# A forgetting-attention layer whose q and k are transposed by VectorE and DMA, in a two-block kernel on one Trainium2 core

## The chip, the core and the metric

The kernel runs on one core of a Trainium2 chip. The metric is device microseconds of one execution, over the whole program. TensorE is called PE in the rows, its weight loads PEld, VectorE DVE, ScalarE ACT, GpSimd POOL and SyncE SP.

## What is computed

A sequence of 256 positions by 1024 channels (float32) goes through five stages. Each weight matrix is used once.

```
x = x + 0.5 * swiglu_ffn(rmsnorm(x, ffn1_norm), ...)          # 1024 -> 2816 -> 1024
x = x + hybrid_mixer(rmsnorm(x, mix_norm), ...)               # 8 heads of 64, banded; and pooling
x = x + 0.5 * swiglu_ffn(rmsnorm(x, ffn2_norm), ...)
x = rmsnorm(x, final_norm)
x = layer_norm(ALPHA * x + fox_mixer(x), ln_g[0], ln_b[0])    # 8 heads of 128, forgetting
x = layer_norm(ALPHA * x + dsa_mixer(x), ln_g[1], ln_b[1])    # 8 heads of 128, indexed top-k
```

The mixer that matters most here, with `scale = 128 ** -0.5`:

```
q, k, v, f_logit, gate = split(x @ w_in)
cum = cumsum(log_sigmoid(f_logit + b_f))            # one decay per head and position
s = q k^T * scale + cum[q] - cum[k], causal
out = (silu(gate) * softmax(s) v) @ w_out
```

## The kernel before, in words

The 256 positions are two tiles (t = 0, 1) of 128 partitions. The activations stand transposed in `xT`, as a high and a low part whose sum is the float32 value. A weight product is therefore three products on PE (`half`, L215): high by high, low by high, high by low. The weights come in 236 units of two blocks of 128 rows and up to 512 columns, in the order of the list `UNITS`. SyncE loads a unit into one of four `raw` buffers (L204), ScalarE casts it to `whi` (L197) and VectorE subtracts to get `wlo` (L198); up to eight units are split ahead of their use.

A chunk (`chunk`, L338) is up to 512 output columns: for each tile 24 products accumulate in one of four PSUM banks called `mm`. Small work is put between the products. `later(us, fn)` and `when(keys, us, fn)` (L136, L140) put a function into a heap with a due time, in a count of PE time (`now`, L168), and each `half` ends by running what is due (`pump`). The due times are in `DUE` (L86). The framework's scheduler sets the final order on every engine, which then works in order.

**Start** (`start`, L1107). Twenty-eight products of zeros (L1120) are issued on PE before the first weights are there.

**Feed-forward layers** (L371). Their hidden values are transposed without PE: VectorE transposes blocks of 32×32 (`hb`, L413), POOL's DMA queue writes `hb` to DRAM in four parts and reads it back as one tile `hd` with the blocks in place (`regroup`, L276), and ScalarE and VectorE make the parts `hh`, `hl` (L239, L240) 9.5 us of counted time later.

**Mixer** (L470). Its four chunks are the pool inputs, k, q and v. The scores of tile 0 (L528) alternate between the heads on partitions 0-63 and 64-127 (`e` = 0, 1). After the softmax each `e` is handled alone: `pv` (L545) transposes its p (four transposes on PE and one copy), and `pv2` (L549) multiplies it with v, 64 columns of v to one half of the output's partitions:

```
for i in range(nh):
    for k in range(nk // P):
        self.mm(aT[t][64 * e:64 * e + 64, j, :], v[k][...], pT[:, i, k, :], ...)
```

The output is then split (`oa`), and products on it follow those on the pool half (`op`).

**Forgetting layer** (`fox`, L687). Its chunks are k (two), the decays with the first part of v, q (two), the rest of v (two), and the gates (in `attend`, L843, where tile 0 goes first). At the layer's start SyncE loads four rows, repeated over 128 partitions: `b_f`, `final_norm`, `ln_g0`, `ln_b0` (L700 to L702). `xT` already holds the normed x up to its row factor, which the evacuations apply (`rs`); x itself, wanted again only in the layer norm at the end, is normed in place right after chunk 0 (L730). In chunk 0 the second half of `xT` is still being made, tile by tile: four transposes on PE, then `xg` on VectorE (L244), a cast on ScalarE (L245), `xl` on VectorE (L246). Each evacuated q or k chunk (`y`, L708) is transposed by PE, four blocks of 128×128 (L713), 1.57 us later; VectorE copies tile 0 (L716) and the parts are made from PSUM (L718). The decays (`cums`, L751) go to DRAM and come back as a row for all partitions on POOL's queue, and POOL adds the causal mask twice (L771, L772). Tile 0's scores use the plain copies (L800), tile 1's the parts.

Of the kernel before, what the change touches and what calls it, by code (L numbers as in the profile page):

```python
# [31 lines left out]
N_WARM = 28  # L32
# [14 lines left out]
def unit_list():  # L47
# [48 lines left out]
    "fox_T": 1.57,  # L96
# [18 lines left out]
class Kern:  # L115
# [332 lines left out]
    def p_T(self, pool, s, nh, nk, split=False):  # L448
# [15 lines left out]
        out = pool.tile([P, 512], F32, name="pT", bufs=2)  # L464
        self.flip = not getattr(self, "flip", False)
        (self.nc.scalar.copy if self.flip else self.nc.vector.tensor_copy)(out, ps)
        return out.rearrange("p (h k q) -> p h k q", h=nh, q=P)


    def mixer(self, u, gain, next_gain):  # L470
        self.stage = "mix"
        nc, tc, A = self.nc, self.tc, self.A
        with tc.tile_pool(name="mix", bufs=1, reuse_waits="tile") as pool:
# [46 lines left out]
            def scores(t, b):  # L520
# [3 lines left out]
                for i in range(nh):  # L524
                    for e in range(2):
                        j, r = nh * b + i, slice(64 * e, 64 * e + 64)
                        if t == 0:
                            self.mm(ps[e][:, i, :], qT[r, j, :], kT[r, j, :], True, True)  # L528
                        else:
                            self.mm3(ps[e][:, i, :], qTs, kTs, True, True, (r, j), (r, j))  # L530
                for e in range(2):
                    s = pool.tile([P, nh, nk], F32, name="s", bufs=6)
                    h0 = 2 * nh * b + e
# [7 lines left out]
                    self.when([("mix", "v")], DUE["mix_pv"], lambda e=e, s=s: pv(t, b, e, s, nh, nk))  # L541
# [3 lines left out]
            def pv(t, b, e, s, nh, nk):  # L545
                pT = self.p_T(pool, s, nh, nk)
                self.later(DUE["mix_pv2"], lambda: pv2(t, b, e, pT, nh, nk))

            def pv2(t, b, e, pT, nh, nk):  # L549
                if b == e == 0:  # L550
# [6 lines left out]
                if e == 1 and nh * (b + 1) == 4:  # L557
# [99 lines left out]
    def silu_gate(self, pool, acc, out, hr):  # L657

        nc = self.nc
        th = pool.tile([P, 512], F32, name="th", bufs=2)  # L660
# [26 lines left out]
    def fox(self, u, gain):  # L687
        self.stage = "fox"
        nc, tc, A = self.nc, self.tc, self.A
        with tc.tile_pool(name="fox", bufs=1, reuse_waits="tile") as pool:  # L690
            kT, qT = (pool.tile([P, 8, P], F32, name=n) for n in ("kT", "qT"))
# [7 lines left out]
            ck0 = pool.tile([P, 8, P], F32, name="ck0")  # L699
# [6 lines left out]
            def qk(acc, t, whole, part, h0, scale):  # L706
# [12 lines left out]
                self.later(DUE["fox_T"], go)  # L719

            def qk_chunks(js):
                nonlocal u
                for j in js:
                    for t, acc in self.chunk(u, 4, gain if j == 0 else None):
                        if j == 0:
# [4 lines left out]
                            nc.vector.scalar_tensor_tensor(self.x[t], self.x[t], rs[t], fg,  # L730
                                                           op0=ALU.mult, op1=ALU.mult)
                        if j < 2:
                            qk(acc, t, kT, [d[:, :, t * P:(t + 1) * P] for d in kTs], 4 * j, rs[t])
                        else:
                            qk(acc, t, qT, qTs if t else None, 4 * j - 8, sr[t])
# [15 lines left out]
            def cums():  # L751
# [12 lines left out]
                nc.scalar.activation(cs, ps[0:8, 0:S], AF.Copy, scale=-1.0)  # L764
                d = self.dp.tile([8, S], F32, name="ck")
# [27 lines left out]
            def scores(t, g):  # L793
# [3 lines left out]
                for i in range(nh):  # L797
                    h = g * nh + i
                    if t == 0:
                        self.mm(ps[:, i, :], qT[:, h, :], kT[:, h, :], True, True)  # L800
                    else:
                        self.mm3(ps[:, i, :], qTs, kTs, True, True, (slice(None), h), (slice(None), h))
                    nc.vector.scalar_tensor_tensor(s[:, i, :], ps[:, i, :], cq[t][:, h:h + 1],
                                                   (ck if t else ck0)[:, h, :], op0=ALU.add, op1=ALU.add)
# [29 lines left out]
            def after(t, o):  # L834
                self.layer_norm(t, o, lg, lb)
# [7 lines left out]
    def attend(self, u, pool, gt, hr, scores, pv):  # L843
# [13 lines left out]
        for t in range(2):  # L857
# [10 lines left out]
            self.open_xT(t)  # L868

# [14 lines left out]
    def dsa(self, u, x_gain=None):  # L884
        self.stage = "dsa"
        nc, tc, A = self.nc, self.tc, self.A
        with tc.tile_pool(name="dsa", bufs=1, reuse_waits="tile") as pool:
# [202 lines left out]
            for t, g in GROUPS:  # L1090
                ql = [("dsa", "ql", i) for i in ((2 * g, 2 * g + 1) if t == 0 else (g,))]
                self.when([("dsa", "sel", t)] + ql, 0.0, lambda t=t, g=g: self.fire(("dsa", "k", t, g)))
            self.attend(u, pool, gt, [None, None], scores, pv)
# [141 lines left out]
```

## Time and profile before

| | |
|---|---|
| median of the runs shown (3) | 724.43 us (723.4 to 725.69) |
| the profiled execution | 723.93 us, span of the profile 722.1 us |
| PE busy | 706.5 us (98%) |
| VectorE, ScalarE busy | 492.1 us (68%), 369.4 us (51%) |
| POOL busy | 62.3 us (9%) |
| moved by DMA | 140.87 MB, 195 GB/s over the span |

The span runs from the first to the last instruction that the profile records; the execution's own time is 1.8 us longer. Matmuls are pipelined and their ends are modelled, so the start of one to the start of the next is the better measure of a product than its duration.

### The profile page before, as it was taken

What the parts mean: (1) busy time and instruction counts of PE and PEld (TensorE: products, weight loads), DVE (VectorE), ACT (ScalarE), POOL (GpSimd) and SP (SyncE); (2) the same over time, 40 slices, a digit from 0 to 9 for tenths busy, and PEclk for the clock granted to TensorE, in tenths of its full rate; (3) what the DMA queues carried; (4) which work ended last, traced back from release to release, by engine and by line L of the source; (5) the groups of instructions that cost most, each with busy time, mean ns of one, the idle gap of its engine ahead of it and who ended that gap; (6) DMA issues with size and microseconds to landing.
All of it is one profiled execution on the core that took longest, in us unless ns stands there. A gap on an engine that the chain in (4) does not pass through costs nothing.

```text
span 722.1 us, 9816 instructions
## 1 busy us (share of the span) xinstructions
PE 706.5 (98%) x3580; PEld 593.9 (82%) x3580; DVE 492.1 (68%) x790; ACT 369.4 (51%) x552; POOL 62.3 (9%) x90
## 2 busy tenths in 40 slices
PE   8999999999999999999999999999999999999995
PEld 7788889888888778888889888778898888778984
DVE  5776765575647867666776575556456968997965
ACT  6654544454545645454454354446464635675820
POOL 0101110300001001011110300000300001000001
PEclk9999999999999999999999999999999999999998
DMA  8898666875734425668765885546572527633501
GB/s 253 305 317 309 212 215 208 285 266 188 271 122 167 154 94 181 202 199 288 228 224 196 270 265 189 196 142 195 169 248 101 156 63 251 206 118 117 175 1 59
DMA packets 42305, 140.87 MB, mean 195 GB/s; under 512 B 5512, under 2 KB 6672, under 8 KB 42128
## 3 DMA queue, kind: packets, MB, share of 16 engines
q1 hardware_dynamic: 37728, 127.23, 52.7%
q0 software_dynamic: 4096, 12.60, 5.1%
q8 instruction: 28, 0.46, 0.2%
q10 hardware_dynamic: 432, 0.41, 0.2%
q14 instruction: 21, 0.17, 0.1%
HBM read 133.39 MB, written 6.82 MB: 194 GB/s over the span
## 4 chain that ended last, share of the span: by engine, by line
PE 88%; DVE 5%; DMA 3%; ACT 2%; issue 1%; SPq 0%; POOL 0%; DVEq 0%; POOLq 0%; ACTq 0%
PE mm L164 79%; PE sc L164 5%; PE tr L179 3%; DVE wlo L198 2%; DMA raw<-in_w 1%; DMA row_final_norm<-in_final_norm 1%; PE tr L164 1%; ACT whi L197 1%; DMA xin<-in_xT 1%; ACT s L445 0%; DVE sel L983 0%; DVE xl L317 0%; DVE sel L992 0%; DVE s L534 0%; POOL hrs L292 0%
## 5 line engine op out<-in xcount | busy, mean ns | idle before, releaser
L198 DVE TENSOR_TENSOR wlo<-raw,whi 128x1024 fp32r<-128x1024 f32 (+3 forms) x236 | 274.6, 1178 | 84.8 <-ACT whi L197 74.9
L197 ACT CAST whi<-raw 128x1024 fp32r<-128x1024 f32 (+3 forms) x236 | 235.7, 1014 | 126.0 <-PE mm L164 76.4
L164 PE MATMUL mm<-whi,xh 128*128 128x512 f32 (+3 forms) x760 | 289.3, 381 | 1.7 <-ACT whi L197 1.6
L164 PE MATMUL mm<-whi,xl 128*128 128x512 f32 (+3 forms) x760 | 284.9, 375 | 2.2 <-DVE xl L246 2.2
L164 PE MATMUL mm<-wlo,xh 128*128 128x512 f32 (+3 forms) x760 | 284.0, 375 | 0.1
L164 PEld LDWEIGHTS mm<-whi,xh 128*128 128x128 f32 x760 | 144.0, 189 | 25.7 <-ACT whi L197 3.0
L164 PEld LDWEIGHTS mm<-whi,xl 128*128 128x128 f32 x760 | 144.2, 190 | 25.0 <-DVE xl L246 2.7
L164 PEld LDWEIGHTS mm<-wlo,xh 128*128 128x128 f32 x760 | 143.9, 189 | 25.3 <-DVE wlo L198 1.3
L164 PE MATMUL mm<-whi,hh 128*128 128x512 f32 x176 | 68.7, 390 | 0.0
L164 PE MATMUL mm<-whi,hl 128*128 128x512 f32 x176 | 68.5, 389 | 0.0
L164 PE MATMUL mm<-wlo,hh 128*128 128x512 f32 x176 | 68.5, 389 | 0.0
L240 DVE TENSOR_TENSOR hl<-hd,hh 128x512 fp32r<-128x512 f32 (+1 forms) x24 | 14.5, 644 | 53.3 <-ACT hh L239 53.3
L239 ACT CAST hh<-hd 128x512 fp32r<-128x512 f32 (+1 forms) x24 | 12.8, 583 | 60.9 <-DMA hd<-d 60.9
L282 POOL DMA_DIRECT2D d<-hb x48 | 26.5, 559 | 149.9 <-DVE hb L413 136.3
L164 PEld LDWEIGHTS mm<-wlo,hh 128*128 128x128 f32 x176 | 33.0, 188 | 6.9
L164 PEld LDWEIGHTS mm<-whi,hh 128*128 128x128 f32 x176 | 33.1, 188 | 6.7
L164 PEld LDWEIGHTS mm<-whi,hl 128*128 128x128 f32 x176 | 33.1, 188 | 6.7
L400 ACT ACTIVATE th<-mm,hr 128x512 f32<-128x512 f32 (+1 forms) x24 | 15.6, 648 | 25.2 <-PE mm L164 24.1
L445 ACT ACTIVATE s<-s,nmax 128x128 f32<-128x128 f32 (+1 forms) x48 | 21.3, 446 | 7.0 <-DVE nmax L443 7.0
L292 POOL TENSOR_TENSOR rs<-ms,mhalf 128x1 f32<-128x1 f32 x10 | 6.5, 653 | 175.4 <-DVE ms L305 175.4
L402 DVE SCALAR_TENSOR_TENSOR a<-th,mm 128x512 f32<-128x512 f32 (+1 forms) x24 | 15.2, 632 | 8.5 <-ACT th L400 8.5
L292 POOL TENSOR_TENSOR lr<-ve,mhalf 128x1 f32<-128x1 f32 x4 | 4.0, 992 | 167.8 <-DVE ve L640 167.8
(219 smaller groups left out, 602.0 us busy)
## 6 DMA issues: line engine op xcount, KB each, us to landing
raw<-in_w SPq DMA_DIRECT2D x208, 512.0 KB, 4.5
d<-hb POOLq DMA_DIRECT2D x40, 128.0 KB, 4.8
hd<-d POOLq DMA_DIRECT2D x10, 512.0 KB, 6.6
raw<-in_w SPq DMA_DIRECT2D x12, 344.0 KB, 3.6
raw<-in_w SPq DMA_DIRECT2D x8, 372.0 KB, 3.6
raw<-in_w SPq DMA_DIRECT2D x8, 256.0 KB, 4.4
x<-in_x SPq DMA_DIRECT2D x2, 512.0 KB, 6.3
B<-in_bias SPq DMA_DIRECT2D x1, 1024.0 KB, 7.0
```

What stands on the lines that cost most here:

```text
L164: self.nc.tensor.matmul(out, a, b, start=start, stop=stop)
L179: self.nc.tensor.transpose(out, a, self.ident[:p, :p])
L197: nc.scalar.copy(hi[:, :m], raw[:, :m])
L198: nc.vector.tensor_sub(lo[:, :m], raw[:, :m], hi[:, :m].bitcast(F32))
L239: nc.scalar.copy(hi, src)
L240: nc.vector.tensor_sub(lo, src, hi.bitcast(F32))
L282: self.nc.gpsimd.dma_start(out=d[a].rearrange("b i m -> i b m"), in_=src[32 * a:32 * a + 32])
L292: self.nc.gpsimd.tensor_tensor(out, a, self.mhalf[:, 0:1].to_broadcast(list(a.shape)), op=ALU.pow)
L400: nc.scalar.activation(th[:, :w], acc[:, :w], AF.Tanh, scale=hr[t])
L402: nc.vector.scalar_tensor_tensor(a[t][:, :w], th[:, :w], 1.0, acc[:, :w], op0=ALU.add, op1=ALU.mult)
L445: nc.scalar.activation(s[:, h, :], s[:, h, :], AF.Exp, bias=m[:, h:h + 1], accum_out=l[:, col + h:col + h + 1])
```

## The change

In the forgetting layer q and k take the way of the feed-forward layers' hidden values: VectorE transposes the evacuated `y` in 32×32 blocks into `yb`, POOL's queue regroups it into `yT` (one buffer for each k chunk, one that both q chunks share), and 12 us of counted time later one function makes what PE's transposes had fed. Tile 0's scores read k from `yT` directly. The final norm of x is put off by 9 us of counted time. Several buffers are shared in time: `final_norm` with `ck0`, `ln_g0` and `ln_b0` with the two `yT` of k, so these two rows are loaded after tile 0's gates (`between`); `pT` with `yb`, `th` with `y`. In the mixer both `e` of a group are handled together, and their products with v alternate. The start has 42 products of zeros.

```diff
-N_WARM = 28
+N_WARM = 42
...
-    "fox_T": 1.57,
+    "fox_T": 12.0,
+    "fox_norm": 9.0,
...
-                    self.when([("mix", "v")], DUE["mix_pv"], lambda e=e, s=s: pv(t, b, e, s, nh, nk))
+                self.when([("mix", "v")], DUE["mix_pv"], lambda: pv(t, b, ss, nh, nk))
...
+            def pv(t, b, ss, nh, nk):
+                pT = [self.p_T(pool, s, nh, nk, bufs=4) for s in ss]
+                self.later(DUE["mix_pv2"], lambda: pv2(t, b, pT, nh, nk))
...
                 for i in range(nh):
                     j = nh * b + i
                     for k in range(nk // P):
-                        self.mm(aT[t][64 * e:64 * e + 64, j, :], v[k][:, 128 * j + 64 * e:128 * j + 64 * e + 64],
-                                pT[:, i, k, :], k == 0, k == nk // P - 1)
+                        for e in range(2):
+                            self.mm(aT[t][64 * e:64 * e + 64, j, :], v[k][:, 128 * j + 64 * e:128 * j + 64 * e + 64],
+                                    pT[e][:, i, k, :], k == 0, k == nk // P - 1)
...
-            fg = self.row(pool, "final_norm")
-            lg, lb = self.row(pool, "ln_g0"), self.row(pool, "ln_b0")
+            fg = self.row(pool, "final_norm", tag="ck0")
...
+            def qk(acc, t, j, scale):
                 y = pool.tile([P, 512], F32, name="y", bufs=2)
                 nc.scalar.activation(y, acc, AF.Copy, scale=scale)
+                if t == 0:
+                    self.yb = pool.tile([P, 4, 256], F32, name="yb", bufs=2)
+                nc.vector.transpose(self.yb[:, :, t * P:(t + 1) * P].rearrange("p b (c j) -> p b c j", c=4),
+                                    y.rearrange("p (c b j) -> p b c j", c=4, b=4))
+                if t == 0:
+                    return
+                yT[j] = pool.tile([P, 4, 256], F32, name=f"yT{j}" if j < 2 else "yTq")
+                self.regroup(yT[j], self.yb)
+                hs = slice(4 * (j % 2), 4 * (j % 2) + 4)
                 def go():
-                    ps = self.bank("tr")
-                    for i in range(4):
-                        self.tr(ps[:, i * P:(i + 1) * P], y[:, i * P:(i + 1) * P])
-                    pv_ = ps.rearrange("p (i q) -> p i q", i=4)
-                    if t == 0:
-                        nc.vector.tensor_copy(whole[:, h0:h0 + 4, :], pv_)
-                    if part is not None:
-                        self.split_psum(*(d[:, h0:h0 + 4, :] for d in part), pv_)
+                    for tt in range(2):
+                        v = yT[j][:, :, tt * P:(tt + 1) * P].rearrange("p a (c j) -> p c a j", c=4)
+                        if j >= 2 and tt == 0:
+                            nc.scalar.copy(qT[:, hs, :].rearrange("p c (a j) -> p c a j", a=4), v)
+                            continue
+                        part = [d[:, hs, tt * P:(tt + 1) * P] for d in kTs] if j < 2 else [d[:, hs, :] for d in qTs]
+                        self.split_psum(*(d.rearrange("p c (a j) -> p c a j", a=4) for d in part), v)
                 self.later(DUE["fox_T"], go)
...
-                            nc.vector.scalar_tensor_tensor(self.x[t], self.x[t], rs[t], fg,
-                                                           op0=ALU.mult, op1=ALU.mult)
+                            self.later(DUE["fox_norm"], lambda t=t: nc.vector.scalar_tensor_tensor(
+                                self.x[t], self.x[t], rs[t], fg, op0=ALU.mult, op1=ALU.mult))
...
+            rows = []
+            self.between = lambda: rows.extend((self.row(pool, "ln_g0", tag="yT0"), self.row(pool, "ln_b0", tag="yT1")))
             self.attend(u, pool, gt, hr, scores, pv)
```

## Rows read from the trace of the kernel before

**Rows 1.** The page: an engine's busy time, and the chain that ended last by engine.
```profile
PE 706.5 (98%) x3580; PEld 593.9 (82%) x3580; DVE 492.1 (68%) x790; ACT 369.4 (51%) x552; POOL 62.3 (9%) x90
PE 88%; DVE 5%; DMA 3%; ACT 2%; issue 1%; SPq 0%; POOL 0%; DVEq 0%; POOLq 0%; ACTq 0%
```
**Rows 2.** The longest of PE's waits: us in total, times, longest.
```profile
PE mm L164 <- DVE xl L246: 2.2, 1, 2.2
```
**Rows 3.** Timeline at the forgetting layer's start: start, us, what, [idle before <- releaser].
```profile
467.78 0.48 PE L164 MATMUL mm<-whi,xh 128*128 128x512 f32 x1
468.54 1.28 DVE L730 SCALAR_TENSOR_TENSOR x<-x,rs,row_final_norm 128x1024 f32<-128x1024 f32 x1 [2.74 <-DMA row_final_norm<-in_final_norm]
469.75 0.69 DVE L246 TENSOR_TENSOR xl<-xg,xh 128x512 fp32r<-128x512 f32 x1
470.49 0.80 PE L164 MATMUL mm<-whi,xl 128*128 128x512 f32 x1 [2.23 <-DVE xl L246]
473.92 0.39 PE L164 MATMUL mm<-whi,xh 128*128 128x512 f32 x1
```
**Rows 4.** Stretches: length; busy us (count) of PE, PEld, DVE, ACT, POOL; clock; DMA share; GB/s.
```profile
467.80:470.50 2.70, 0.47 (x5) 0.16 (x2) 1.96 (x3) 0.36 (x1) 0.00 (x0) 0.97 0.85 338
470.50:473.90 3.40, 3.40 (x8) 2.71 (x9) 3.40 (x5) 0.62 (x1) 0.00 (x0) 0.52 0.52 172
474.00:496.00 22.00, 22.00 (x118) 19.19 (x117) 10.80 (x15) 12.17 (x17) 0.00 (x0) 1.00 0.52 166
615.00:720.00 105.00, 97.99 (x565) 83.04 (x563) 86.62 (x226) 54.38 (x109) 2.84 (x4) 0.98 0.34 114
```
**Rows 5.** The chain in the forgetting layer's projections: one group of transposes.
```profile
519.59 0.44 PE tr L179 x4
```
**Rows 6.** The mixer: timeline of PE, the chain (start, us, what), a stretch.
```profile
258.13 1.09 PE L164 MATMUL sc<-pT,v 128*64 128x128 f32 x8
235.86 1.16 PE L164 MATMUL sc<-kT,qT 64*128 64x128 f32 x16
...
255.41 1.51 PE sc L164 x16
...
262.50:267.15 4.65, 4.65 (x22) 3.86 (x21) 3.44 (x4) 3.67 (x5) 0.00 (x0) 1.00 0.15 33
```
**Rows 7.** The kernel's start: timeline of PE, two stretches, the chain.
```profile
1.01 3.17 PE L1120 MATMUL tr<-zero 128*128 128x128 bf16 x28 [1.01 <-DVE zero L1139]
5.27 0.79 PE L164 MATMUL mm<-whi,xh 128*128 128x512 f32 x1 [1.09 <-ACT whi L197]
...
5.30:9.45 4.15, 4.15 (x10) 3.28 (x11) 2.73 (x7) 2.65 (x8) 0.00 (x0) 1.00 0.95 304
18.50:22.85 4.35, 3.59 (x13) 2.02 (x13) 3.39 (x6) 3.14 (x4) 0.00 (x0) 1.00 0.98 386
...
14.22 6.20 DMA raw<-in_w
```
**Rows 8.** First feed-forward layer: last transpose, writes, the cast that waits; PE beside.
```profile
59.71 0.71 DVE L413 STREAM_TRANSPOSE hb<-h 128x512 f32<-128x512 f32 x1
60.72 2.19 POOL L282 DMA_DIRECT2D d<-hb  x4 [17.25 <-DVE hb L413]
73.08 1.14 ACT L239 CAST hh<-hd 128x512 fp32r<-128x512 f32 x2 [6.80 <-DMA hd<-d]
...
66.10:73.10 7.00, 7.00 (x33) 5.79 (x32) 1.45 (x2) 0.20 (x2) 0.76 (x1) 1.00 0.85 328
```
**Rows 9.** The gathered tile hd: its reads' time from issue to landing.
```profile
DMA to landing us min/median/max: 3.1/6.3/7.7
```
**Rows 10.** Timeline: the decays' last addition, the last q, tile 0's last scores.
```profile
517.45 2.40 POOL L772 TENSOR_TENSOR ck<-ck,cst 128x1024 f32<-128x1024 f32 x1
...
523.28 0.68 ACT L708 ACTIVATE y<-mm,qr 128x512 f32<-128x512 f32 x1
...
544.17 0.63 PE L164 MATMUL sc<-kT,qT 128*128 128x128 f32 x4
```

More of the change, by code (lines that the diff above doesn't have):

```diff
@@ L446, in softmax_part, with p_T @@
                                  accum_out=l[:, col + h:col + h + 1])
-    def p_T(self, pool, s, nh, nk, split=False):
+    def p_T(self, pool, s, nh, nk, split=False, bufs=2):
         ps = self.bank("tr")
@@ L463, in p_T @@
                 self.tr(v[:, h, k, :], s[:, h, k * P:(k + 1) * P])
-        out = pool.tile([P, 512], F32, name="pT", bufs=2)
+        out = pool.tile([P, 512], F32, name="pT", tag="yb" if self.stage == "fox" else "pT", bufs=bufs)
         self.flip = not getattr(self, "flip", False)
@@ L530, in scores @@
                             self.mm3(ps[e][:, i, :], qTs, kTs, True, True, (r, j), (r, j))
+                ss = []
                 for e in range(2):
                     s = pool.tile([P, nh, nk], F32, name="s", bufs=6)
+                    ss.append(s)
                     h0 = 2 * nh * b + e
@@ L540, in scores, with pv2 @@
                         nc.vector.tensor_scalar(s[:, i, :], s[:, i, :], ri[:, i:i + 1], None, op0=ALU.mult)
-                    self.when([("mix", "v")], DUE["mix_pv"], lambda e=e, s=s: pv(t, b, e, s, nh, nk))
+                self.when([("mix", "v")], DUE["mix_pv"], lambda: pv(t, b, ss, nh, nk))
             aT = {}
[L545 to L550, printed above, removed]
+            def pv(t, b, ss, nh, nk):
+                pT = [self.p_T(pool, s, nh, nk, bufs=4) for s in ss]
+                self.later(DUE["mix_pv2"], lambda: pv2(t, b, pT, nh, nk))
+            def pv2(t, b, pT, nh, nk):
+                if b == 0:
                     aT[t] = self.bank("sc").rearrange("p (i q) -> p i q", i=4)
@@ L554, in pv2 @@
                     for k in range(nk // P):
-                        self.mm(aT[t][64 * e:64 * e + 64, j, :], v[k][:, 128 * j + 64 * e:128 * j + 64 * e + 64],
-                                pT[:, i, k, :], k == 0, k == nk // P - 1)
-                if e == 1 and nh * (b + 1) == 4:
+                        for e in range(2):
+                            self.mm(aT[t][64 * e:64 * e + 64, j, :], v[k][:, 128 * j + 64 * e:128 * j + 64 * e + 64],
+                                    pT[e][:, i, k, :], k == 0, k == nk // P - 1)
+                if nh * (b + 1) == 4:
                     self.split_psum(*oT[t, "a"], aT[t])
@@ L659, in silu_gate @@
         nc = self.nc
-        th = pool.tile([P, 512], F32, name="th", bufs=2)
+        th = pool.tile([P, 512], F32, name="th", tag="y" if self.stage == "fox" else "th", bufs=2)
         nc.scalar.activation(th, acc, AF.Tanh, scale=0.5 if hr is None else hr)
@@ L690, in fox @@
         with tc.tile_pool(name="fox", bufs=1, reuse_waits="tile") as pool:
-            kT, qT = (pool.tile([P, 8, P], F32, name=n) for n in ("kT", "qT"))
+            yT = {}
+            qT = pool.tile([P, 8, P], F32, name="qT")
             kTs, qTs = self.parts(pool, [P, 8, S], "kTs"), self.parts(pool, [P, 8, P], "qTs")
@@ L764, in cums @@
                 nc.scalar.activation(cs, ps[0:8, 0:S], AF.Copy, scale=-1.0)
+                ck0 = self.ck0 = pool.tile([P, 8, P], F32, name="ck0", tag="ck0")
                 d = self.dp.tile([8, S], F32, name="ck")
@@ L803, in scores @@
                     nc.vector.scalar_tensor_tensor(s[:, i, :], ps[:, i, :], cq[t][:, h:h + 1],
-                                                   (ck if t else ck0)[:, h, :], op0=ALU.add, op1=ALU.add)
+                                                   (ck if t else self.ck0)[:, h, :], op0=ALU.add, op1=ALU.add)
                 self.softmax_part(pool, s, nh, nk, l[t], g * nh)
@@ L834, in after @@
             def after(t, o):
-                self.layer_norm(t, o, lg, lb)
+                self.layer_norm(t, o, *rows)
                 if t == 0:
@@ L868, in attend @@
             self.open_xT(t)
+            if t == 0:
+                self.between()
     def gate_out(self, t, hb, o, l, f, gt):
@@ L1092, in dsa @@
                 self.when([("dsa", "sel", t)] + ql, 0.0, lambda t=t, g=g: self.fire(("dsa", "k", t, g)))
+            self.between = lambda: None
             self.attend(u, pool, gt, [None, None], scores, pv)
```

9 lines of the change are left out of this document (4 added, 5 removed).

## The prediction

> **What bounds the kernel now.** I read the page first. The product engine (PE) is busy 98% of the span of 722.1 us, and the chain that ended last is 88% PE [rows 1]: time can go only where PE waits, runs at the lower clock, or does something that can be left out. PE's list of waits comes next; the longest, 2.2 us, is a weight product that waits for VectorE's xl [rows 2]. The timeline shows why. At the start of the forgetting layer VectorE stands 2.74 us before the final norm of x (L730), because the row of gains is still landing. The norm takes 1.28 us, and only behind it comes xl, for which PE stands [rows 3]. Then the clock: in the next 3.4 us it is 0.52 of full, 1.2 instead of 2.4 GHz, after a stretch in which PE was busy 0.47 of 2.70 us [rows 4]. I then looked up the other operations that the change touches: the transposes by PE [rows 5], the mixer's products with v [rows 6], the first 23 us [rows 7], and the way by VectorE and DMA, which the feed-forward layers already use [rows 8, 9].
>
> The sum is made against the profiled execution's own 723.93 us, which is 0.50 under the median of the runs shown, 724.43; I add 0.5 at the end. About 0.3% (2.2 us) is what a measurement of this kernel can tell from no change.
>
> **1. Final norm put off.** The norm leaves VectorE's queue between xg and xl, and with it the wait for the row. xl then follows its cast and is done before the product that needs it, which starts one step after 467.78. A step is 0.228 us, so it starts at 468.01 instead of 470.49: 2.48 us of standing go. From 470.49 to 473.92 are eight steps in 3.43 us; at 0.228 each they are 1.82, so the low clock cost 1.61 [rows 3]. Together **−4.09**. Late next is tile 1's xl: its transposes end at about 468.0, then xg, cast and xl at 0.69 or less each, so 470.1; it is needed twelve products after 467.78, at 470.5. It fits, barely. The two norms come about 9 us later, beside weight products, where VectorE is busy 10.80 of 22 us [rows 4]: nothing. The rows ln_g0 and ln_b0 leave SP's queue at the layer's start and stand in it between weight loads, after the gates of tile 0. Their buffers are those of k, last read by tile 0's scores, at 544 [rows 10]; SP is behind that, so it does not wait, and the weights behind it lie eight units ahead. Nothing.
>
> **2. q and k transposed by VectorE and DMA.** Removed from PE: eight groups of four transposes, 0.44 us each on the chain [rows 5]: **−3.5**. VectorE loses four copies and gets eight transposes of 0.71 [rows 8], at most 5.7 us in a stretch of some 60 in which it is half idle [rows 4]: hidden by PE's products. ScalarE gets two copies of q, about 0.6 each like the cast of the gathered tile [rows 8]: hidden too. POOL gets 16 writes and 4 reads, and their way is the term to bound. In the feed-forward layer the last transpose starts at 59.71, the writes are issued from 60.72, and ScalarE starts on the result at 73.08: 13.4 us, 14.1 with an evacuation of 0.68 before it. ScalarE stood 6.8 us for it, and PE did not stand: busy 7.00 of 7.00 us [rows 8], since the weights are cast eight units ahead. In the new place k has all the time it needs. The last q is the close one: its evacuation starts at 523.28 and its score products at 544.17 [rows 10], 20.9 us later, 20.4 with one group of transposes gone. Against 14.1 that leaves 6 us. But POOL is also busy with the row of decays until 519.85 [rows 10]. If the first q queues behind that, it lands 12.4 later (60.72 to 73.08), at 532. The two q share one buffer, so the second read waits for the first's parts, some 2.5 us: issued at 535, it lands by the median of 6.3 us [rows 9] at 541, copied by 542. Slack 1.5 us or more. Bounds: 0; or, with the longest landing of 7.7 [rows 9] at each of three transfers, a stand of 1 to 3 us and the clock's fall after it, together 4. I take **0**: the nearest row is ScalarE's wait of 6.8 us, which cost PE nothing.
>
> A rule speaks against this part. The Trainium skill, VectorE: DVE Perf Modes, Rules for kernel authors, gives a 128×128 transpose to TensorE if it may end in PSUM. By that rule the 3.5 would be no gain, and the sum would be 717.7. On the rows PE is the scarce engine and VectorE half idle there, so I go by the rows.
>
> **3. Heads take turns at v.** There are 24 products of 128×64 by 128 columns, recorded as 48 instructions. One group of eight, all to the same 64 partitions, lasts 1.09 us [rows 6]. After the change neighbours write partitions 0-63 and 64-127. Two rows are near. The scores of tile 0 use row halves in turn, and sixteen last 1.16 us, hardly more than eight. And where now two groups with v meet, one to the upper and one to the lower half, sixteen take 1.51 on the chain [rows 6], though two groups alone would take two times 1.09: where they meet, column halves seem to run beside each other. So I take half of the steps away: a step within a group is about 0.11 us ((1.09 − 0.3) / 7), 24 × 0.11 = **−2.6**. Bounds: 0 if neighbours don't overlap in this order; −3.0 if fewer changes between kinds of products save too. Is PE the limit there? After the last product with v PE is busy 4.65 of 4.65 us with products on the pool half, before those on the attention half begin [rows 6]; the split that these wait for is a cast and a subtraction, under 1.4 us. So PE is the limit, with 3 us of cover.
>
> **4. 42 warming products.** 28 take 3.17 us, so fourteen more take 1.6 and end at 5.8, where the first weight product now starts at 5.27 after a gap of 1.09: 0.5 late. If the low clock ended earlier, the ten products until 9.45 would save 0.2 each [rows 7]. Neither reaches the end: the chain from 14 to 20.4 is one weight transfer of 6.20 us, with the DMA engines 98% busy, and PE is busy only 3.59 of 4.35 us before 22.85 [rows 7]: it stands for weights anyway. **0**; bounds +0.5 and −1.
>
> Sum: −4.09 − 3.5 − 2.6 = −10.2; 723.93 − 10.2 = 713.7; with 0.5 added **714.2 us**. Later stages only shift: in the last 105 us the DMA engines are busy 0.34 [rows 4], and what VectorE does there starts with PE's products.
>
> **The rivals.**
> *Column halves don't overlap in this order.* Against it stands the group of sixteen. Part 3 is 0: 716.8. Chance 0.06.
> *The last q lands late.* One stand before the scores of tile 0, priced like the one at the layer's start, 4.09: 718.3. For it: POOL's queue and the single buffer; against: 1.5 us of slack and gate products that can go first. Chance 0.16.
> *The earlier clock counts.* PE has a gap before 5.27 and ten products at the lower clock after it. If the clock rose earlier and an earlier PE brought the next transfers forward, the 0.8 us that PE stands before 22.85 would go: 713.4. Against: that chain holds no product. The Trainium skill, TensorE: Matmul & The Clock Gate, What's actually happening, says that activity releases the lower clock; no row here shows it rise sooner. Chance 0.04.
> *Nothing arrives.* The norm is put off, but its row or the gathered parts stop VectorE again at the same cost: 723 to 725. Chance 0.03.
> *Slower.* Place: ScalarE's queue in the projections. The parts of q and k stand in it from their due time on; if each waits longer than the weights are cast ahead, PE stands four times, at 4.09 each +16.4: 730.6. Eight units of six products at 0.228 are 11 us; with the 12 of the due time that decides at a landing 23 us after the evacuation, and I count 14 to 18. Chance 0.07.
>
> **How the numbers follow.** My forecast has 0.64; its own range is 712.5 to 716. The range reaches over the columns and a late q, 711.8 to 719.5; the last two rivals and the edges are left out. Faster by over 0.3%: 0.64 + 0.06 + 0.16 + 0.04 = 0.90; within: 0.03; slower: 0.07.
>
> **What would show it.** Right: no wait for xl at the layer's start and a clock of 1.00 there; no transposes of y on PE; the sixteen products of a pair with v in about 1.1 us; casts of q and k that wait for a gather while PE goes on. Wrong: a wait of PE for qT before tile 0's scores, v's products still 0.11 apart, VectorE standing for the gains' row in another place, or a later stage that now waits where it did not.

## The result, and the profile after

The kernel after the change takes 728.32 us (median of 6 runs), the kernel before 723.91 on the same chip: ratio 1.0063, 95% interval 1.0037 to 1.0088. It is 4.4 us slower where 10.2 faster was forecast. Its profiled execution took 729.85 us (span 728.1), 1.5 above its median.

The page shows it first: PE is busy 2.7 us less, as its transposes of q and k are gone and the mixer's products overlap, but it is a smaller part of the chain, 72% instead of 88% [rows 1].

```profile
PE 703.8 (97%) x3562; PEld 589.6 (81%) x3562; DVE 497.5 (68%) x794; ACT 368.5 (51%) x554; POOL 74.5 (10%) x110
PE 72%; DMA 12%; DVE 7%; ACT 3%; issue 3%; POOL 2%; SPq 0%; DVEq 0%; POOLq 0%; ACTq 0%
```

PE's list of waits after (total, times, longest) is headed by two waits that were not there before [rows 2]; both are of tile 0's scores in the forgetting layer.

```profile
PE sc L165 <- ACT qT L729: 4.9, 1, 4.9
PE sc L165 <- DVE s L819: 1.8, 1, 1.8
PE mm L165 <- DVE a L403: 1.7, 2, 1.0
PE mm L165 <- ACT whi L198: 1.7, 2, 1.3
PE mm L165 <- DVE xl L247: 1.3, 1, 1.3
```

**Where the time went.** The table takes the start of one and the same instruction in two traces and gives what each stage took more (+) or less than in the trace of before. The stages end, in the time of before, with the first feed-forward layer (190.8), the mixer (279.9), the second feed-forward layer (461.7), the first evacuated k (474.9), the second tile's decay logits (498.3), the last evacuated q (523.3), the last gate of the forgetting layer (573.1) and the last x (713.7). The ratio is the measured one, to the kernel before on the same chip, with its 95% interval; it can differ a little from that of the two medians. e1 to e18 are the experiments; each has one trace, and where its profiled execution lies above or below the median, so does the sum of its row.

| | median | ratio | ffn1 | mixer | ffn2 | first k | decays | last q | last gate | rest |
|---|---|---|---|---|---|---|---|---|---|---|
| after | 728.32 | 1.0063 (1.0037-1.0088) | +1.7 | -2.5 | +1.4 | -2.4 | -1.7 | -1.7 | **+11.3** | +0.6 |
| e1 | 717.89 | 0.9930 (0.9906-0.9954) | 0.0 | -2.5 | +1.1 | -2.4 | -1.6 | -0.3 | 0.0 | +2.2 |
| e2 | 724.25 | 1.0021 (1.0001-1.0041) | -0.5 | -2.5 | +1.4 | -2.6 | -1.7 | -1.7 | +8.2 | +1.0 |
| e3 | 720.92 | 0.9971 (0.9952-0.9989) | -1.3 | -2.5 | +2.5 | -0.2 | 0.0 | 0.0 | 0.0 | +0.4 |
| e4 | 724.09 | 1.0018 (1.0003-1.0034) | +0.1 | 0.0 | 0.0 | -0.3 | 0.0 | 0.0 | 0.0 | +0.3 |
| e5 | 725.36 | 1.0021 (1.0002-1.0040) | +1.1 | -2.6 | 0.0 | -2.4 | -1.6 | -1.7 | +9.1 | +0.3 |
| e6 | 728.77 | 1.0067 (1.0048-1.0085) | +1.0 | -2.5 | 0.0 | -2.5 | -1.7 | -1.7 | +11.3 | +1.0 |
| e7 | 720.81 | 0.9960 (0.9941-0.9979) | +0.2 | -2.5 | 0.0 | -2.4 | -1.7 | -1.7 | +4.5 | +2.6 |
| e8 | 717.52 | 0.9906 (0.9873-0.9938) | +2.4 | -2.5 | 0.0 | -4.0 | -2.3 | +0.3 | 0.0 | +0.8 |
| e9 | 715.99 | 0.9906 (0.9881-0.9931) | -0.5 | -2.5 | +0.6 | -4.0 | -2.1 | +0.2 | +0.4 | +1.1 |
| e10 | 718.20 | 0.9931 (0.9906-0.9956) | +3.7 | -2.5 | 0.0 | -4.0 | -2.3 | +0.3 | 0.0 | +2.1 |
| e11 | 721.52 | 0.9975 (0.9956-0.9994) | +0.4 | 0.0 | 0.0 | -4.0 | -0.1 | -0.1 | 0.0 | +2.6 |
| e12 | 717.04 | 0.9917 (0.9888-0.9946) | +2.0 | -2.5 | 0.0 | -4.0 | -2.3 | -1.1 | +2.6 | +2.1 |
| e13 | 724.31 | 1.0013 (0.9995-1.0031) | +1.9 | 0.0 | 0.0 | -2.6 | +0.2 | 0.0 | 0.0 | +1.2 |
| e14 | 724.03 | 1.0000 (0.9985-1.0015) | +0.1 | 0.0 | 0.0 | -2.4 | +0.2 | 0.0 | 0.0 | 0.0 |
| e15 | 717.59 | 0.9919 (0.9888-0.9950) | +3.3 | -2.5 | 0.0 | -4.0 | -2.0 | -1.2 | +0.4 | +1.2 |
| e16 | 727.16 | 1.0041 (1.0021-1.0061) | +2.5 | -2.5 | 0.0 | -2.1 | -1.7 | -1.7 | +10.6 | +2.1 |
| e17 | 724.77 | 1.0014 (0.9994-1.0034) | +1.7 | -2.5 | 0.0 | -2.3 | -1.6 | -1.4 | +10.4 | +0.8 |
| e18 | 723.77 | 0.9990 (0.9965-1.0014) | +1.8 | -2.5 | 0.0 | -4.0 | -1.8 | -1.2 | +8.7 | +1.4 |

Read the first row: by the last q the change is 5.2 us ahead, though it began 1.7 behind; then 11.3 us go in one stage. What stands in the first column is mostly chance: e8 and e10 are one and the same kernel and differ by 1.2 there.

**The stage that loses.** Timelines after (start, us, what, [idle before <- releaser]): POOL, then ScalarE and VectorE, then PE.

```profile
509.08 0.57 POOL L283 DMA_DIRECT2D d<-yb  x1 [0.61 <-DVE yb L717]
513.92 2.39 POOL L786 TENSOR_TENSOR ck<-ck,cst 128x1024 f32<-128x1024 f32 x1 [4.27 <-DMA ck<-ck]
516.28 3.02 POOL L787 TENSOR_TENSOR ck<-ck,cst 128x1024 f32<-128x1024 f32 x1
519.25 1.65 POOL L283 DMA_DIRECT2D d<-yb  x3
526.39 0.76 POOL L284 DMA_DIRECT2D yTq<-d  x1 [5.49 <-DMA d<-yb]
534.10 0.76 POOL L284 DMA_DIRECT2D yTq<-d  x1 [4.78 <-DVE qTsl L241]
...
531.94 0.62 ACT L729 COPY qT<-yTq 128x512 f32<-128x512 f32 x1 [8.76 <-DMA yTq<-d]
539.84 1.04 ACT L198 CAST whi<-raw 128x1024 fp32r<-128x1024 f32 x1 [2.10 <-DMA raw<-in_w]
541.41 1.04 ACT L198 CAST whi<-raw 128x1024 fp32r<-128x1024 f32 x1 [0.52 <-DMA raw<-in_w]
542.36 0.61 ACT L729 COPY qT<-yTq 128x512 f32<-128x512 f32 x1
...
544.90 1.22 DVE L199 TENSOR_TENSOR wlo<-raw,whi 128x1024 fp32r<-128x1024 f32 x1 [0.59 <-ACT whi L198]
546.05 0.60 DVE L819 SCALAR_TENSOR_TENSOR s<-sc,cq,ck 128x128 f32<-128x128 f32 x2
...
535.34 0.50 PE L165 MATMUL mm<-wlo,xh 128*128 128x512 f32 x1 [0.53 <-DVE wlo L199]
537.73 0.38 PE L165 MATMUL sc<-yT,qT 128*128 128x128 f32 x2
543.02 0.79 PE L165 MATMUL sc<-yT,qT 128*128 128x128 f32 x2 [4.91 <-ACT qT L729]
546.44 1.22 PE L165 MATMUL sc<-yT,qT 128*128 128x128 f32 x4 [1.77 <-DVE s L819]
```

Three of the first q's four writes stand on POOL behind the decays' additions; its read goes out at 526.39. ScalarE stands 8.76 us for it, in front of the casts of the weights that come next. When it goes on, the weights are late in turn: it waits 2.10 and 0.52 us for raw ones, and the copy of the last q, which had landed by 538.5 (issued at 534.10, 4.4 us, the tile's own row below), stands behind these casts until 542.36. PE stands from 538.1. Then the additions of the first scores stand on VectorE behind a low part of weights (544.90), and PE stands once more. The chain that ended last runs through the same pieces (start, us, what):

```profile
526.39 5.52 DMA yTq<-d
533.08 0.96 ACT whi L198
535.21 1.23 DVE wlo L199
536.45 4.86 DMA raw<-in_w
541.41 1.04 ACT whi L198
546.05 0.35 DVE s L819
546.44 1.22 PE sc L165 x4
```

So the weights that come late were asked for late: a load waits until a buffer of raw weights has been cast and subtracted, and SyncE issued none between 524.46 and 535.31. In 530 to 535 the DMA engines were busy 0.40, in the kernel of e1, which has no such stand, 0.77. Stretches and tile (columns as in [rows 4]):

```profile
DMA to landing us min/median/max: 4.4/5.0/5.5
...
538.10:543.00 4.90, 0.01 (x1) 0.00 (x0) 2.64 (x3) 2.64 (x4) 0.00 (x0) 0.83 0.98 374
543.00:551.00 8.00, 6.20 (x21) 5.10 (x22) 4.77 (x10) 3.84 (x5) 0.00 (x0) 0.50 0.62 205
```

PE stands 4.9 + 1.8 us, and 0.5 before them for a low part of weights; from 543 it works 6.20 us at half the clock, which at full clock would be some 3.1. Together 10.3 of the 11.3.

**The layer's start** (against [rows 3]): tile 0's norm is still between xg and xl.

```profile
468.17 1.28 DVE L744 SCALAR_TENSOR_TENSOR x<-x,rs,row_final_norm 128x1024 f32<-128x1024 f32 x1 [1.85 <-DMA row_final_norm<-in_final_norm]
469.38 0.69 DVE L247 TENSOR_TENSOR xl<-xg,xh 128x512 fp32r<-128x512 f32 x1
470.12 0.50 PE L165 MATMUL mm<-whi,xl 128*128 128x512 f32 x1 [1.34 <-DVE xl L247]
```

**The mixer and the first 23 us** (against [rows 6, 7]): sixteen products of a pair with v last what eight did; the first weight product is at the full clock, and PE stands for weights as before.

```profile
256.79 1.09 PE L165 MATMUL sc<-pT,v 128*64 128x128 f32 x16
...
6.03 0.50 PE L165 MATMUL mm<-whi,xh 128*128 128x512 f32 x1 [0.42 <-ACT whi L198]
...
18.50:22.85 4.35, 3.46 (x14) 2.52 (x15) 2.96 (x3) 2.69 (x4) 0.00 (x0) 1.00 1.01 383
```

### The profile page after: what moved, and what is told of

Its sections match the earlier page's. It is cut to its first block, busy times and chain, and to the rows that moved or that the text cites. A ratio compares the mean times of both kernels' runs of the same rounds, so it can differ in the third digit from the quotient of the medians.

```text
span 728.1 us, 9833 instructions
## 1 busy us (share of the span) xinstructions
PE 703.8 (97%) x3562; PEld 589.6 (81%) x3562; DVE 497.5 (68%) x794; ACT 368.5 (51%) x554; POOL 74.5 (10%) x110
## 4 chain that ended last, share of the span: by engine, by line
PE 72%; DMA 12%; DVE 7%; ACT 3%; issue 3%; POOL 2%; SPq 0%; DVEq 0%; POOLq 0%; ACTq 0%
PE mm L165 63%; PE sc L165 5%; DMA raw<-in_w 5%; DVE wlo L199 3%; PE tr L180 3%; DMA hd<-d 2%; DMA d<-hb 2%; ACT whi L198 2%; DMA ck<-ck 1%; POOL d L283 1%; PE tr L165 1%; DMA yTq<-d 1%; DMA d<-yb 1%; DMA row_final_norm<-in_final_norm 1%; ACT s L446 0%
## 5 line engine op out<-in xcount | busy, mean ns | idle before, releaser
L199 DVE TENSOR_TENSOR wlo<-raw,whi 128x1024 fp32r<-128x1024 f32 (+3 forms) x236 | 277.9, 1191 | 75.3 <-ACT whi L198 72.1
```

Source lines behind the costliest of these rows:

```text
L199: nc.vector.tensor_sub(lo[:, :m], raw[:, :m], hi[:, :m].bitcast(F32))
```

## The experiments

**e1.** The kernel after, with q (not k) back on PE:

```diff
+                if j >= 2:
...
+                    self.later(1.57, go_pe)
+                    return
```

> The kernel after the change, but its four evacuated q chunks are transposed by PE again (1.57 us later, as before); k stays on the way by VectorE and DMA, and the rest of the change stays. Theory: nearly all that the change lost lies at one place, PE's stand for the last q before tile 0's scores (4.9 us for qT, 1.8 for s behind it, and the low clock that follows; from the last q's evacuation, 5.3 us ahead of the kernel before, to the second gate chunk of tile 0, 5.6 behind it). Without it 11 us come back and four groups of transposes, 1.8 us, are paid again: 728.3 - 11 + 1.8 = 719, about 5 us under the kernel before, no wait for qT in PE's list, and PEclk full from 540 to 560. Rival: the stand only holds a place for work that is late anyhow (weights, decays); then PE stands there for something else and the time stays at 724 or above.

717.89 us, 10.4 less than after (9.6 by the two ratios). The stage to the last gate loses nothing, no wait for qT is left. So the loss belongs to q's new way alone; k's costs nothing.

**e2, e5, e6: POOL's queue and the buffer.** Decays' additions on VectorE (e2); behind the first q's writes (e5); a second buffer (e6):

```diff
-                nc.gpsimd.tensor_tensor(ck0, ck[:, :, 0:P], diag, op=ALU.add)
+                nc.vector.tensor_tensor(ck0, ck[:, :, 0:P], diag, op=ALU.add)
...
                 self.regroup(yT[j], self.yb)
+                if j == 3:
+                    self.add()
...
-                yT[j] = pool.tile([P, 4, 256], F32, name=f"yT{j}" if j < 2 else "yTq")
+                yT[j] = pool.tile([P, 4, 256], F32, name=f"yT{j}")
```

> The kernel after the change, but the two additions of the causal mask to the decays are done by VectorE and no longer stand in POOL's queue. Theory: the first q is late because three of its four writes stand behind these additions (13.9 to 19.3 after 500 us), and the last q because its read waits until the one buffer of q is free. With the additions away the writes of the first q are issued at about 509 to 511, it lands by 522, the last one (evacuated at 518) by about 532, 10 us earlier than the 541 of the trace; PE is then not waiting, and the time falls by the stand and its low clock, to 717 to 719. Rival a: the landing times are set by the DMA engines, which the weights keep busy; then the last q lands at 538 or later, PE stands again, and the time is 724 or above. Rival b: VectorE now stands for the decays' rows (they land at 513.9) with two additions of 1 to 2.4 us ahead of the weights' low parts; PE then waits for wlo around 515 to 520 and the gain is smaller, 720 to 723.

724.25, the time of rival a, and near its landing: the first q's read went out at 517.9, the last one's at 530.1, which took 7.1 us, and PE stood 3.2 for qT and 3.4 for s. Of rival b only VectorE's stand came, 7.70 us for the decays' rows; PE waited for no low part between 505 and 530.

> The kernel after the change, but the two mask additions to the decays are issued after the last q's transfers are ordered, so that on POOL they stand behind all four writes of the first q instead of ahead of three of them. Theory: POOL's queue is the cause of the late q. The first q's read then goes out when the additions end, at about 519 instead of 526.4, lands at 525; the last q (evacuated at 518) is written by 522, read at 527, lands at 533 to 534. PE reaches tile 0's scores at 538: no stand, no low clock after it, 728.3 - 11 = 717. Rival: the transfers are slow because the DMA engines carry the weights at the same time (with the additions on VectorE the writes took 6 to 8 us to land); the last q lands at 537 or later, PE stands 2 to 4 us and the time is 720 to 724.

725.36, slower than theory and rival. Half of the theory held: the reads go out 5.5 and 5.7 us earlier than after, and the last q has landed by 532.8, before PE comes at 535. Still its copy starts only at 537.35, and 9.1 of 11.3 us are lost: ScalarE has come to the first q's copy earlier and stands even longer for it (its timeline):

```profile
526.23 0.62 ACT L731 COPY qT<-yTq 128x512 f32<-128x512 f32 x1 [9.47 <-DMA yTq<-d]
```

> The kernel after the change with a buffer of its own for each of the two gathered q (they shared one). Theory: POOL's queue, not the buffer, sets the landing: the writes of the last q go out only from 527.1, behind the first one's read, and take some 5 us to land, so its read goes out at 532 to 534 instead of 534.1 and PE still stands 3 to 5 us: 726 to 728. Rival: the read waits mainly for the buffer; with its own it goes out at 530, lands at 536 to 537, PE does not stand and the time is 718 or less.

728.77, and 5.1 us of standing for qT: the buffer is not the cause.

**e7.** Tile 0's scores later:

```diff
-    "fox_s": (2.04, 2.43, ...
+    "fox_s": (9.0, 9.4, ...
```

> The kernel after the change with the due times of tile 0's two groups of scores raised from 2.04 and 2.43 to 9.0 and 9.4 us, so that PE has the 24 products of the first gate chunk (5.5 us) ahead of them. Theory: the loss is a matter of order on PE: what stands behind qT's score products in PE's queue was ready. With them later PE does not stand for qT: 728.3 - 11 = 717 to 719. Rival: ScalarE stands 8.8 us for the gathered q with the casts of the gates' weights behind it, so PE now stands for whi or wlo in the gate chunks, 2 to 5 us, with the low clock after it: 721 to 726.

720.81. PE no longer stands for q, but in this stage 1.1 us for a cast and 1.1 for low parts of weights, behind ScalarE's stand of 9.76, and the clock falls there too (0.67 and 0.76 in 533 to 536 and 536 to 539). Of the 11.3 us 4.5 are left: theory and rival share it.

**e16, e17, e18: the last links cleared.** The last q's copy on POOL (e16); with e5's and e6's edits (e17); with the norm held back too (e18):

```diff
-                            nc.scalar.copy(qT[...], v)
+                            (nc.gpsimd.tensor_copy if j == 3 else nc.scalar.copy)(qT[...], v)
```

> The kernel after the change, but the plain copy of the last q's tile 0 out of the gathered buffer is made by POOL, whose queue is empty then, instead of ScalarE. Theory: the gathered q was there at about 538.5 (read issued at 534.1, 4.4 us), just when PE came to it at 538.1; that PE stood until 543.0 is ScalarE's queue: two casts that wait 2.1 and 0.5 us for raw weights stand ahead of its copy. POOL copies it by 540; PE stands 1.5 to 2 us instead of 4.9 and the time falls by 3 to 6 us, to 722 to 725. Rival: the transfer itself lands at 541 to 542; PE stands 4 us or more as before, 727 to 728.

> As e16, and the two mask additions behind the first q's writes, and a buffer for each q: every queue that the last q passed is cleared. In e5 the last q's read was issued at 528.4 and landed by 533.7 while PE came at 535 and ScalarE copied it only at 537.4. Theory: with its own buffer and POOL's copy it is there by 533 to 534, PE does not stand for qT and the stage from the last q's evacuation to the last gate loses 0 to 3 us instead of 11.3: 728.3 - 9 = 717 to 720. Rival: the additions of the scores on VectorE or the casts of the gates' weights, held up by ScalarE's stand of 9 us for the first q, stop PE 3 us or more with the low clock after it: 721 to 725.

> The kernel of e17 with the final norm held back as in e8: the change as it was meant, with the queues cleared and 42 products of zeros. Theory: 1.6 us less than e17 and, with the transposes of k and q off PE (3.4 us) and no stand, the 714 of the prediction plus what the last layer gives back: 714.5 to 716.5, under e9 and e10 (716.0 and 718.2), which pay for q on PE. Rival: no better than those, 717 or more, since the first q still holds ScalarE.

727.16, 724.77, 723.77. In e16 the wait for qT fell to 1.4 us as expected and in e17 it is gone, but the time did not come: the stage loses 10.6 and 10.4 us as before. In e16 the wait for s grew from 1.8 to 5.4 us, so its rival has the time right without its cause, as the last q had landed by 538.7. The rival of e17 holds, and that of e18. The waits of e17, then ScalarE and VectorE:

```profile
PE sc L165 <- DVE s L825: 7.8, 1, 7.8
...
528.38 0.62 ACT L731 COPY qT<-yT 128x512 f32<-128x512 f32 x1 [10.66 <-DMA yT<-d]
537.00 1.04 ACT L198 CAST whi<-raw 128x1024 fp32r<-128x1024 f32 x1 [2.37 <-DMA raw<-in_w]
540.30 0.61 ACT L240 CAST qTsh<-yT 128x512 fp32r<-128x512 f32 x1
...
538.08 1.22 DVE L199 TENSOR_TENSOR wlo<-raw,whi 128x1024 fp32r<-128x1024 f32 x1 [2.51 <-ACT whi L198]
541.56 0.68 DVE L241 TENSOR_TENSOR qTsl<-yT,qTsh 128x512 fp32r<-128x512 f32 x1
542.17 2.35 DVE L199 TENSOR_TENSOR wlo<-raw,whi 128x1024 fp32r<-128x1024 f32 x2
544.44 0.60 DVE L825 SCALAR_TENSOR_TENSOR s<-sc,cq,ck 128x128 f32<-128x128 f32 x2
```

The scores are there by 536.6, but their additions stand on VectorE behind low parts of weights, which wait for casts, which wait for weights that ScalarE's stand of 10.66 us held up. Whoever is freed first, PE waits for the next in the same tail. In the traces of after, e5, e16 and e17 the chain that ended last passes the first q's read and ScalarE, as above. In e18, which still loses 8.7 us, it does not (start, us, what):

```profile
528.17 1.23 DVE wlo L199
529.42 6.87 DMA raw<-in_w
536.39 1.05 ACT whi L198
```

There a load of weights is itself slow, 6.87 us where 4.86 stand above, and the last q's read, issued at 528.85, is there only at 536.2; in e2 it is two loads of 7.93 and 6.05. So there seem to be two ways to the same tail: ScalarE's stand for the first q, and transfers of weights and of q that are slow at the same time. That either is the root is read from these rows and from e1, where ScalarE has no such stand and q no transfers; it isn't tested by itself, as a version with the copies put behind the casts was not tried.

**e3, e4.** The mixer alone on the kernel before, then the 42 products alone:

```diff
-                    self.when(..., lambda e=e, s=s: pv(t, b, e, s, nh, nk))
+                self.when(..., lambda: pv(t, b, ss, nh, nk))
...
-N_WARM = 28
+N_WARM = 42
```

> The kernel before, with one part of the change: in the mixer both halves of the heads are transposed together and their products with v alternate. Theory: neighbours that write different partition halves run beside each other; sixteen products take 1.1 us on the trace of the changed kernel where two groups of eight took 2.2, and the stage from the first scores to the last evacuation lost 2.5 us there. So 723.9 - 2.5 = 721.4. Rival: it is given back in a later stage, which waits for weights or VectorE: 723.9.

720.92: 2.3 us faster. The 2.5 come in the mixer in every kernel that has the edit. Some traces give 0.6 to 2.5 back in the next feed-forward layer, where PE stands for VectorE (1.2 and 0.7 us in e3); others with the same edit give back nothing.

> The kernel before, with one part of the change: 42 instead of 28 products of zeros at the start. The trace of the changed kernel is 0.3 us behind at the first tanh, 0.6 at 25 us and 1.8 at 60 us, with the clock full from the first weight product on. Theory: the clock rises earlier, but PE then stands for weights; worth 0: 723.9 within 1, and what was lost by 60 us is chance in the transfers. Rival: the later start of the first products holds up the casts and the buffers of raw weights behind them, and the 1.8 us are its price: 725.7, with PE 1.5 us or more behind the kernel before at 60 us.

724.09, 0.8 more (0.2 to 2.5).

**e13, e14.** `N_WARM = 14` and `70` on the kernel before.

> The kernel before with 14 products of zeros instead of 28. Theory: the number of these products is worth nothing by itself, the start is set by the weights' transfers: 723.2 within 0.7, although the low clock lasts longer at the start. Rival: what e4 (0.8 more with 42) and e9 beside e10 (2.2 less with 28) point to is a price of each product at the start; then 14 is faster than 28 by about as much, 722 to 722.5.

> The kernel before with 70 products of zeros: PE's first weight product comes at about 9.0 instead of 5.3 us. Theory: PE has no 3.7 us to give at the start, since it stands only 0.8 of the first 23 us and is otherwise busy; it makes up part at the full clock (ten products at half the time, 2 us) and loses the rest: 725. If the order of the first products, which is another with 42 and 70 than with 28, costs by itself, 726 or more. Rival: the transfers of weights hide it all: 723.2 to 724.

724.31 and 724.03 beside 723.46: no trend with the count. The rival of e13 is out, and its theory nearly holds (0.85 where 0.7 was allowed, but the interval has 1 in it). In e14 the rival comes nearest: its ratio is 1.0000, though the first weight product comes at 7.14 us instead of 5.27 (9.0 had been expected). So the 0.8 of e4 doesn't grow with the products; it is read as chance.

**e8, e10, e11: the norm really held back**, on e1's kernel (e8, e10) and alone on the kernel before (e11):

```diff
-                            self.later(DUE["fox_norm"], ...)
...
+                nc.vector.scalar_tensor_tensor(rh, zf[:, t, 0:1], 0.0, rs[t], op0=ALU.mult, op1=ALU.add)
+                nc.vector.scalar_tensor_tensor(self.x[t], self.x[t], rh, fg, op0=ALU.mult, op1=ALU.mult)
```

> The kernel of e1 (after the change, q by PE), with the final norm of x made to depend on the decays' logits of its tile (its row factor gets zero times a logit added), so that it cannot be done before 494 us. Theory: the change put the norm off in the list of due times only; on VectorE the norm of tile 0 still stands between xg and xl, waits 1.85 us for the row of gains and costs PE 1.34 us. Held back, xl follows its cast, PE does not wait for xl, and the stage is 1.5 to 1.7 us shorter: 717.9 - 1.6 = 716.3, the 4.09 of the prediction in full. Rival: xl is late by itself (transposes, xg, cast and xl in a row); PE waits for it 1 us or more as before and the time stays at 717.9.

717.52. In every kernel with it the first k comes 4.0 us earlier. VectorE and a stretch in e8:

```profile
466.15 0.69 DVE L247 TENSOR_TENSOR xl<-xg,xh 128x512 fp32r<-128x512 f32 x1 [0.42 <-ACT xh L246]
...
466.00:470.00 4.00, 4.00 (x21) 3.31 (x20) 3.57 (x5) 2.17 (x4) 0.00 (x0) 1.00 0.57 177
```

xl follows its cast, PE is busy throughout at the full clock: the theory in its place. In the whole time it is less clear, 0.4 us under e1 by the medians and 1.7 by the ratios, and e10, the same kernel again, is no faster than e1.

> The kernel of e8 once more, with more runs and on the same chip as e9, e11 and e12. The sum by the parts measured in their stages is 723.2 - 2.5 (mixer) - 4.0 (norm) - 1.7 (k) = 715.0, and what later stages give back (1 to 2.5 us between the mixer and the forgetting layer, up to 2 in the last layer) makes it 716 to 718.

718.20, just above the 716 to 718 expected.

> The kernel before with one edit: the final norm of x is held back behind the decays' logits (its row factor gets zero times a logit added). Theory: term 1 of the prediction is right in size and only did not happen in the change: PE's wait for xl (2.2 us) and the low clock behind it are gone, the first k is evacuated 4.1 us earlier, 723.2 - 4.1 = 719.1. Rival a: without the norm xl still comes 1 us late: 720.5. Rival b: the 4 us are given back in the last layer, where VectorE is busy over 9.8 of 10 us: 721 to 723.

721.52, 1.7 us faster: the theory in its place, -4.0, and rival b by half: the last layer took 2.6 us more in this trace.

**e9, e12, e15: which version is best.** e9 is e8 with 28 products; e12 has q by DMA with the edits of e5, e6, e7 and e8; e15 is e12 with 28.

> The kernel of e8 (mixer in turn, k by VectorE and DMA, q by PE, norm held back) with 28 products of zeros instead of 42. Beside e10, which is the same with 42. Theory: the fourteen products are worth nothing, since the first 23 us are set by the transfers of weights: the two agree within 0.5 us, at 717 to 718. Rival: e4 alone measured 0.8 us more with 42 (0.2 to 2.5); then this one is 0.8 faster than e10, with its first tanh and the 60 us point that much earlier.

> The kernel after the change with all that the earlier runs suggest for its own way of q: the norm held back, the two mask additions behind the first q's writes, a buffer for each q, tile 0's scores 7 us later. Theory: with PE not standing for q any more, the two groups of transposes per q that PE is spared are a gain over e10: 717 - 1.8 = 715. Rival: ScalarE's queue decides; it stands some 9 us for the first gathered q with the casts of the gates' weights behind it, PE then waits for whi and wlo 1 to 3 us with the low clock after it, as in e7, and the time is 717 to 720, no better than e10.

> The kernel of e12 with 28 products of zeros instead of 42. If the fourteen cost 1 to 1.5 us, as e4 and the points at 60 us of all traces suggest (0.7 behind with 42, 0.8 ahead with 28), this is 715.5 to 716, level with e9 at 716.0. Rival: it is chance; then 717.0 as e12.

715.99, 717.04, 717.59; their intervals overlap with e10's. e9 is 2.2 us under e10 where its theory allowed 0.5 and its rival said 0.8; since e13 and e14 show no trend and e15 with 28 is no faster than e12, the distance is read as chance in the first layer (-0.5 and +3.7 in their traces), which no run shows. e12's rival holds: no better than with q on PE. e8 and e9 beat the kernel before by 0.9% (0.6 to 1.3), e10, the kernel of e8, by 0.7%; q on PE is the simpler way to it.

## Why the prediction was wrong

**Term 2, q and k: the step that failed** is "Bounds: 0; or ... together 4. I take 0", with ScalarE's wait of 6.8 us as the nearest row. PE was relieved as reckoned: 1.7 us for k, 1.7 for q, 3.4 of 3.5. But the waits cost 11.3. The slack of 1.5 us set the landing of the last q against its scores at 544.17 [rows 10], on the clock of the kernel before. But that row is not the first: the first pair of scores already reads both q, as the heads of the two groups alternate on PE, and in the trace of before it stands 1.9 earlier (first line below); PE came earlier still, mostly by the gains of the forecast itself, at 538.1; and ScalarE's queue added 3.9 between landing and copy. POOL's part of the count was good: reads forecast at 535, seen at 534.10.

The size failed too. A late q was priced like one stand, 4.09; it brought three waits and 8 us at half the clock. And ScalarE's queue, the place of the slower rival, was the right place: that rival was to decide at a landing 23 us after the evacuation, and 14 to 18 were counted, though term 2 itself has the first q landing at 532, which is 20.6 after its evacuation in the trace of before (second line). After the change its copy started at 531.94, 24.8 us after its evacuation at 507.16. It got 0.07; the rival of the late q, 0.16, named the place where PE stood but not what lay behind it. In the feed-forward layer ScalarE's wait of 6.8 us cost nothing, as PE was busy throughout [rows 8]; that nothing on PE needed, soon after, what stood behind it on ScalarE is the reading, not a test.

```profile
542.22 0.60 PE L164 MATMUL sc<-kT,qT 128*128 128x128 f32 x4
...
511.42 0.68 ACT L708 ACTIVATE y<-mm,qr 128x512 f32<-128x512 f32 x1
```

By the rule cited in term 2 (the Trainium skill, VectorE: DVE Perf Modes, Rules for kernel authors) a 128x128 transpose goes to TensorE where it may end in PSUM. For q the runs agree with it (e1 against after, 10.4 us), for k they don't: its four groups came off PE for 1.7 us and nobody waited.

**Term 1, the norm**: "The norm leaves VectorE's queue between xg and xl" is what failed. A due time sets where a function enters the program, and the scheduler still put tile 0's norm between them; only tile 1's moved. The size of the term was right: -4.0 once it was held back (e8, e11) against -4.09. The -2.4 of the change isn't owed to the norm's due time: VectorE still waits for the row of gains, 1.85 us instead of 2.74, and the clock doesn't fall. The rows ln_g0 and ln_b0 no longer come beside that row (in the two us up to 470 the DMA engines moved 370 GB/s before and 30 after), which may be why; it isn't shown, since e13 and e14, with the layer unedited, have -2.6 and -2.4 too, and e3 and e4 only -0.2 and -0.3. All eight traces with this edit as it stands have -2.1 to -2.6. So the stage of before, from which 4.09 was reckoned, is at the dear end of its own spread; against e13 and e14 the norm held back is worth 1.4 and 1.6.

**Term 3, the heads in turn**, held: -2.5 against -2.6, column halves run beside each other. **Term 4**, 0, held: at 7.3 us the products already came in steps of 0.23 us, where before they took 0.43 until 9.3, and the rival that this would count did not come. (The clock column of [rows 7] has 1.00 there for before; the lower clock is read from these steps.)

**Later stages only shift** held by half. The last layer took up to 2.6 us more: e1 is 5.7 us ahead at the last gate and 3.6 at the end. VectorE is busy 9.9 of 10 us there (620 to 630 before), and PE stands up to 1.9 us for its y. But it isn't simply an earlier PE that pays: e14, 2.1 us ahead, kept all of it, and e16, 5.1 behind, lost 2.1 more.

## What to carry to other kernels

When a change makes the bottleneck engine faster, measure every slack against its new, earlier arrival, and ask of each in-order queue that a late transfer passes what stands behind the waiting instruction, not only who waits for its result. A wait of 6.8 us cost nothing in one stage; one of 8.8 came with a loss of 11.3 in another, where the next weights and the next consumer stood behind it. And a due time isn't a place in a queue: look where the instruction really stands, or make it depend on something late.

## What the runs showed that was not expected

After the stand of 4.9 us the clock stayed at 1.2 GHz until 551, 8 us in which PE was busy 6.20. At the layer's start it fell in the three traces where PE had stood 2.23, 2.00 and 1.84 us for xl (before, e3, e4) and not where it had stood 1.28 and 1.13 (e14, e13), nor after the change, where it had stood 1.34.

VectorE and POOL slowed each other. The same subtraction takes 0.87 us alone; beside POOL's second addition in e16 (timeline) it took 3.07, which is until that addition ends (521.39) and not quite 0.87 more; and the addition took 3.05 where before 2.40 stands [rows 10]. The pieces look as if one waited for the other's whole instruction. After the change this held up the last q too: evacuated at 518.04, it was transposed at 521.53, behind the four subtractions of the last line. It did not decide the landing there, as POOL came to its writes only at 527.14.

```profile
519.05 3.07 DVE L199 TENSOR_TENSOR wlo<-raw,whi 128x688 fp32r<-128x688 f32 x1
518.34 3.05 POOL L788 TENSOR_TENSOR ck<-ck,cst 128x1024 f32<-128x1024 f32 x1
...
514.09 7.52 DVE L199 TENSOR_TENSOR wlo<-raw,whi 128x688 fp32r<-128x688 f32 x4 [0.44 <-ACT whi L198]
```
